# Four buffers for the modulation's weight loads, and its VectorE steps tied to the weight tile they accompany

## Chip, cores and metric

One core of one Trainium2 chip. The metric is the device time of one execution in microseconds (us), median of the runs shown. TensorE (PE) does matmuls, VectorE (DVE) and ScalarE (ACT) elementwise work, GpSimd (POOL) elementwise work and, here, the issue of some DMAs, SyncE (SP) the issue of the others. Each engine works through its own instructions strictly in the order in which they were emitted.

## The reference, cut to what matters

Two transformer blocks over 512 tokens of width 1024, in float32. The part around the change is the conditioning of the second block: for each of its two layers a vector `c` of 1024 numbers gives six modulation vectors of 1024 numbers each.

```python
cond = jax.nn.silu(c)
for i in range(DEPTH):                      # DEPTH = 2
    mod = cond @ ada_w[i] + ada_b[i]        # (1, 1024) @ (1024, 6144)
    sh1, sc1, g1, sh2, sc2, g2 = jnp.split(mod, 6, axis=-1)
    h = modulate(rmsnorm(x, norm1_g[i]), sh1, sc1)
    ...
def sq_relu_mlp(xn, w_up, w_down):
    return jnp.square(jax.nn.relu(xn @ w_up)) @ w_down
```

`ada_w` depends on nothing that the first block computes, so this product can be made at any time before the second block.

## The kernel before

The residual stream is held transposed in eight tiles `h0` to `h7` of 128x512. A weight matrix comes in tiles of 128x1024 (512 KB). For each of them SP issues the load into `wr` (two buffers), ACT makes a rounded copy `wh`, DVE the remainder `wl = wr - wh` (three buffers each), and PE does 24 matmuls of 128x512 (8 blocks of the contraction, each as `xh*wh`, `xl*wh` and `xh*wl`) into one PSUM bank. "Weight tile" below means these 24 matmuls with what belongs to them.

`mlp` (line 675) runs four rounds of 8 up tiles and 8 down tiles, 64 in all. After an up tile DVE computes `t` from PSUM, ACT squares it to `a` and rounds it to `ah`, and DVE makes `al = a - ah`; the eight pairs `ah`, `al` are the moving operands of the following down tiles. After a down tile DVE adds the PSUM bank to `h`. There are four such MLPs; the first two carry a side job.

The side job is `ada` (line 1236), a generator. The matrix `ada_w[i]` has 48 tiles of 128x1024: six groups `q` of eight row blocks `k`. For each, POOL issues a load into an `adaw` buffer (the pool's two), and DVE does two instructions on 128x512 that add `adaw * cs` to the accumulator `ada`. After the eighth of a group DVE transposes `ada` into another `adaw` buffer and reduces it into `red`. At the end 16 small DMAs bring `red` into `part`, and DVE reduces that to `mod`. `mlp` calls the generator once per weight tile, but not at every eighth (`step`, line 681); what is left runs before the last down tiles.

These calls only record instructions. The order in which each engine gets them is made afterwards by `Sched.order` (line 274): a list scheduler that works through estimated times (`cost`, line 243) and, at each moment when an engine is free, hands it the ready instruction that was recorded first. An `ada` step is ready there as soon as its load has landed by those estimates, whatever weight tile PE is at. `Sched.after` (line 194) adds one artificial predecessor, the instruction recorded last, to everything recorded inside it; before, one place in the third layer uses it. All instructions are emitted at line 414, so that they all carry this line in the profile and are told apart by their tiles.

Of the kernel before, what the change touches and what calls it, by code (L numbers as in the profile page):

```python
# [14 lines left out]
ALU = mybir.AluOpType  # L15
AX = mybir.AxisListType
PSUM = bass.MemoryType.PSUM

P = 128
S = 512  # L20
D = 1024
HALVES = slice(0, S // 2), slice(S // 2, S)
KD = D // P
# [15 lines left out]
V_BS = 208  # L39
V_QG, V_KG = 224, 226  # L40
NV = 228


class View:
# [110 lines left out]
class Sched:  # L155
# [37 lines left out]
    @contextmanager  # L193
    def after(self):

        self.gate = len(self.ops) - 1
        yield
        self.gate = None

# [42 lines left out]
    @staticmethod  # L242
    def cost(o, outs, ins):

        ps = any(x.tile.pool.space is not None for x in ins)
        if o.name == "dma_start":
            x = (outs + ins)[0]
            return 1000 if o.eng == "gpsimd" else 60, 1550 + (x.box[1] - x.box[0]) * x.size * 4 / 360
        n = max(x.size for x in outs + ins) if o.name in ("tensor_reduce", "bn_stats", "bn_aggr", "max") else outs[0].size
        if o.eng == "tensor":  # L250
            x = outs[0].size
            if o.name == "matmul" and ins[0].tile.dt == F32:
                return max(64, 4 * 0.42 * x), 200
            return max(107 if o.name == "transpose" else 54, 0.417 * x + 2.5), 200
        if o.eng == "scalar":
            aps = sum(isinstance(o.kw.get(k), View) for k in ("bias", "scale", "accum_out"))
            return (51 if ps else 93) + 0.834 * n + 93 * max(0, aps - 1) + (60 if aps == 1 else 0), 130
        if o.eng == "gpsimd":
            if o.name == "tensor_scalar":
                return 160 if n < 16 else 244 + 0.834 * n, 130  # L260
            if o.name == "memset":
                return 100, 130
            return (300 + 164 * n if n < 16 else 100 + 2.2 * n), 130
        c = 68 + 1.042 * n
        if o.name == "scalar_tensor_tensor" and isinstance(o.args[2], View):
            c += 61
        if o.name == "tensor_scalar" and not ps:
            c = 130 + 0.52 * n
        if o.name == "reciprocal":
            c = 70 + 6.3 * n  # L270
        return c, 130
# [219 lines left out]
class Net:  # L491
# [744 lines left out]
    def ada(self, i):  # L1236
        nc, I = self.nc, self.I

        def side(pool):
            m = self.mod[i]  # L1240
            red, part = (self.t(pool, x, [P, 4, 6 * KD], bufs=1) for x in ("red", "part"))
            for q in range(6):
                acc = self.t(pool, "ada", [P, D])
                for k in range(KD):
                    w = self.t(pool, "adaw", [P, D])
                    nc.gpsimd.dma_start(w, I["ada_w"][i, k, :, q * D : (q + 1) * D])
                    c = self.cs[:, k : k + 1]
                    for s in (0, 512):
                        a = acc[:, s : s + 512]
                        if k == 0:  # L1250
                            nc.vector.tensor_scalar(a, w[:, s : s + 512], c, 1.0, ALU.mult, ALU.mult)
                        else:
                            nc.vector.scalar_tensor_tensor(a, w[:, s : s + 512], c, a, ALU.mult, ALU.add)
                    if k < KD - 1:
                        yield

                tr = self.t(pool, "adaw", [P, D])
                nc.vector.transpose(tr, acc)
                nc.vector.tensor_reduce(red[:, :, q * KD : (q + 1) * KD], tr.rearrange("p (j a k) -> p a j k", a=4, k=32), AX.X, ALU.add)
                yield  # L1260
            for a in range(4):
                for g in range(4):
                    nc.gpsimd.dma_start(part[32 * a : 32 * a + 32, g, :], red[32 * g : 32 * g + 32, a, :])
                yield
            nc.vector.tensor_reduce(m, part.rearrange("p g k -> p k g"), AX.X, ALU.add)
            nc.vector.tensor_tensor(m, m, self.vec[:, V_ADAB[i] : V_ADAB[i] + 48], ALU.add)
            for col, g in ((8, V_N1[i]), (32, V_N2[i])):
                nc.vector.scalar_tensor_tensor(m[:, col : col + 8], m[:, col : col + 8], 1.0, self.vec[:, g : g + 8], ALU.add, ALU.mult)

        return side  # L1270
# [8 lines left out]
    def build(self):  # L1279
        nc, I = self.nc, self.I  # L1280
        self.vec = self.t(self.per, "vec", [P, NV])
        nc.sync.dma_start(self.vec, I["vec"])
# [60 lines left out]
def _consts():  # L1343
    f = np.float32
    half = 32
    inv = 1.0 / (10000.0 ** (np.arange(0, HD, 2, dtype=f) / f(HD)))
    ang = np.arange(S, dtype=f)[:, None] * inv[None, :].astype(f)
    sign = np.concatenate([-np.ones(half, f), np.ones(half, f)])

    def table(a):  # L1350
        c, s = np.cos(a).astype(f).T, np.sin(a).astype(f).T
        c = np.concatenate([c, c])
        s = np.concatenate([s, s]) * sign[:, None]
        return np.stack([np.concatenate([c, c]), np.concatenate([s, s])]).astype(f)

    t = np.arange(S)
    row = (t // 64 - (S // 64) // 2).astype(f)
    col = (t % 64 - 32).astype(f)
    fr = (f(10000.0) ** (-np.arange(16, dtype=f) / f(16))).astype(f)
    ang2 = np.concatenate([row[:, None] * fr, col[:, None] * fr], axis=-1).astype(f)  # L1360
    causal = np.zeros((P, S), f)
    causal[:, S - P :] = np.where(np.arange(P)[None, :] <= np.arange(P)[:, None], 0.0, FAR)
    tri = np.zeros((P, S + 3 * P), f)
    tri[:, 3 * P :] = (np.arange(P)[:, None] <= np.arange(S)[None, :]).astype(f)
    esel = np.zeros((P, 2), f)
    esel[64] = esel[96] = 1.0
    return {"rope_a": table(ang), "rope_c": table(ang2), "causal": causal, "tri": tri, "esel": esel, "ident": np.eye(P, dtype=f)}


def _layout(a):  # L1370
# [61 lines left out]
    r["vec"] = cat(cols, 1)  # L1432
    assert r["vec"].shape == (P, NV)
    r.update(_consts())
# [15 lines left out]
```

## Time and profile before

| | |
|---|---|
| median of 3 runs | 2618.81 us (2616.95 to 2618.96) |
| the profiled execution | 2615.0 us, its span 2613.2 us |
| PE busy | 2544.9 us (97%), 12614 matmuls |
| DVE busy | 1582.8 us (61%) |
| ACT busy | 1169.8 us (45%) |
| POOL busy | 406.6 us (16%) |
| DMA | 290.47 MB, mean 111 GB/s |
| granted TensorE clock, mean | 0.992 |
| `ada` multiply-adds on DVE | 192, from 265.5 to 1050.0 us |
| `adaw` loads | 96 of 512 KB, from 226.3 to 1044.8 us |

The two MLPs with the side job begin near 263 and near 876 us in the span; the other two fill most of the stretches from 1500 to 1800 and from 2300 to 2600 us. In a row of the timeline stand the start, the duration, the engine, the operation with its output and inputs, and in brackets how long the engine had been idle before and what ended that. A matmul's duration overlaps with the next one's, so a rate is read from starts or from counts. In the table of stretches the number in parentheses is the count of instructions.

### The profile page before, as it was taken

The numbers are of one execution on the slowest core, as the hardware profiler recorded it, in microseconds if no ns is written. First come the engines' busy times: TensorE is split into PE (matmuls) and PEld (weight loads), VectorE is DVE, ScalarE is ACT, GpSimd is POOL, SyncE is SP. The second block draws the span as 40 slices with busy tenths as digits, with TensorE's granted clock in tenths as the row PEclk, the third lists the DMA queues.
The fourth block names the chain that finished last, engine by engine and source line by source line (L and its number), as shares of the span: only waits on it lengthen the run. The fifth ranks groups of instructions, "written<-read, shape, count | busy, mean of one in ns | idle before, by whom it ended". The sixth has DMA issues, their size and how long they took to land.

```text
span 2613.2 us, 33470 instructions
## 1 busy us (share of the span) xinstructions
PE 2544.9 (97%) x12614; PEld 2127.2 (81%) x12614; DVE 1582.8 (61%) x2629; ACT 1169.8 (45%) x2104; POOL 406.6 (16%) x453
## 2 busy tenths in 40 slices
PE   7999998999999998999999999999999999999999
PEld 6779786888888886888877888888888888888887
DVE  7998877445578778535698644435447654644433
ACT  5677322335488423324687523323425443523322
POOL 3741112000054111100541200001102110200000
PEclk9999998999999999999999999999999999999999
DMA  4222676333222577332310232222333322233232
GB/s 149 89 69 90 223 227 198 99 96 106 93 74 62 177 231 230 113 97 82 97 57 25 89 97 97 97 97 94 109 105 117 101 95 91 90 99 97 98 97 94
DMA packets 90419, 290.47 MB, mean 111 GB/s; under 512 B 12401, under 2 KB 15729, under 8 KB 90257
## 3 DMA queue, kind: packets, MB, share of 16 engines
q1 hardware_dynamic: 75408, 237.80, 28.3%
q0 software_dynamic: 14848, 50.54, 6.1%
q8 instruction: 99, 1.62, 0.2%
q14 instruction: 64, 0.52, 0.1%
HBM read 277.28 MB, written 2.10 MB: 107 GB/s over the span
## 4 chain that ended last, share of the span: by engine, by line
PE 77%; DVE 10%; DMA 7%; ACT 3%; issue 3%; POOL 0%; SPq 0%; DVEq 0%; ACTq 0%; POOLq 0%
PE mm L414 65%; DMA adaw<-in_ada_w 6%; PE lg L414 4%; PE tp L414 4%; PE po L414 3%; DVE ada L414 2%; DVE mask L414 1%; DVE wl L414 1%; DVE st L414 1%; DVE acc L414 1%; ACT wh L414 0%; DVE xl L414 0%; DVE y L414 0%; DVE o L414 0%; DVE pr L414 0%
## 5 line engine op out<-in xcount | busy, mean ns | idle before, releaser
L414 ACT ACTIVATE wh<-wr 128x1024 fp32r<-128x1024 f32 (+2 forms) x472 | 446.2, 951 | 1022.2 <-PE mm L414 847.3
L414 PE MATMUL mm<-xh,wh 128*128 128x512 f32 (+1 forms) x1640 | 625.7, 382 | 8.3 <-ACT wh L414 8.3
L414 DVE TENSOR_TENSOR wl<-wr,wh 128x1024 fp32r<-128x1024 f32 (+1 forms) x374 | 448.3, 1199 | 301.9 <-ACT wh L414 295.1
L414 PE MATMUL mm<-xh,wl 128*128 128x512 f32 (+1 forms) x1640 | 625.5, 382 | 5.4 <-DVE wl L414 4.8
L414 PE MATMUL mm<-xl,wh 128*128 128x512 f32 (+1 forms) x1640 | 625.0, 381 | 0.7 <-POOL xl L414 0.7
L414 PE MATMUL mm<-ah,wh 128*128 128x512 f32 (+1 forms) x1072 | 409.8, 382 | 13.7 <-ACT ah L414 13.7
L414 PE MATMUL mm<-al,wh 128*128 128x512 f32 (+1 forms) x1072 | 409.8, 382 | 3.6 <-DVE al L414 3.6
L414 PE MATMUL mm<-ah,wl 128*128 128x512 f32 (+1 forms) x1072 | 408.4, 381 | 0.6 <-DVE wl L414 0.6
L414 PEld LDWEIGHTS mm<-xh,wl 128*128 128x128 f32 x1640 | 311.3, 190 | 63.2 <-DVE wl L414 7.7
L414 PEld LDWEIGHTS mm<-xh,wh 128*128 128x128 f32 x1640 | 310.7, 190 | 62.4 <-ACT wh L414 8.7
L414 PEld LDWEIGHTS mm<-xl,wh 128*128 128x128 f32 x1640 | 311.4, 190 | 56.3 <-POOL xl L414 1.4
L414 PEld LDWEIGHTS mm<-ah,wh 128*128 128x128 f32 x1072 | 202.7, 189 | 54.2 <-ACT ah L414 15.8
L414 PEld LDWEIGHTS mm<-al,wh 128*128 128x128 f32 x1072 | 202.7, 189 | 44.5 <-DVE al L414 6.2
L414 DVE SCALAR_TENSOR_TENSOR h<-mm,mod,h 128x512 f32<-128x512 f32 (+1 forms) x113 | 79.9, 708 | 261.8 <-PE mm L414 261.6
L414 PEld LDWEIGHTS mm<-ah,wl 128*128 128x128 f32 x1072 | 202.8, 189 | 39.1 <-DVE wl L414 1.0
L414 POOL TENSOR_TENSOR wl<-wr,wh 128x512 fp32r<-128x512 f32 x98 | 132.5, 1362 | 220.6 <-ACT wh L414 215.8
L414 DVE SCALAR_TENSOR_TENSOR ada<-adaw,cs,ada 128x512 f32<-128x512 f32 x168 | 119.5, 748 | 72.5 <-DMA adaw<-in_ada_w 72.3
L414 ACT ACTIVATE pr<-pr,mn 128x128 f32<-128x128 f32 (+2 forms) x192 | 116.7, 610 | 21.0 <-DVE mn L414 20.2
L414 DVE TENSOR_TENSOR h<-mm,h 128x512 f32<-128x512 f32 (+1 forms) x91 | 56.3, 623 | 108.3 <-PE mm L414 108.2
L414 ACT ACTIVATE ah<-a 128x512 fp32r<-128x512 f32 x128 | 81.0, 632 | 83.8 <-DVE a L414 81.7
L414 DVE TENSOR_TENSOR al<-a,ah 128x512 fp32r<-128x512 f32 x128 | 88.2, 691 | 42.8 <-ACT ah L414 42.8
L414 PE MATMUL tp<-ident,pr 128*128 128x128 f32 x576 | 110.0, 277 | 1.9 <-ACT pr L414 1.0
(260 smaller groups left out, 3795.8 us busy)
## 6 DMA issues: line engine op xcount, KB each, us to landing
adaw<-in_ada_w POOLq DMA_DIRECT2D x96, 512.0 KB, 4.5
wr<-in_w_up SPq DMA_DIRECT2D x64, 512.0 KB
wr<-in_w_down SPq DMA_DIRECT2D x64, 512.0 KB
wr<-in_w_in SPq DMA_DIRECT2D x64, 512.0 KB
wr<-in_w_out SPq DMA_DIRECT2D x64, 512.0 KB
wr<-in_w_gu SPq DMA_DIRECT2D x24, 512.0 KB
wr<-in_w_gv SPq DMA_DIRECT2D x24, 512.0 KB
wr<-in_w_go SPq DMA_DIRECT2D x32, 384.0 KB
```

The costliest lines, as they stand in the source:

```text
L414: getattr(getattr(self.nc, o.eng), o.name)(*args, **kw)
```

## The change

It has three parts. `adaw` gets four buffers (`AW`) in place of the pool's two. A new `Sched.paced(i)` makes instruction `i` a predecessor of what is recorded inside; the multiply-adds of an `ada` step, and the transpose and reduction, are recorded inside it, with `g`, the last instruction recorded before the step. At an up tile that is the DVE instruction that makes `al`, at a down tile the DVE addition to `h`; where a transpose follows directly on the eighth step, it is that step's last instruction. The loads are recorded outside of it. In the scheduler's estimates a DMA issued by POOL now takes 600 ns of POOL (1000 before) and lands 2000 ns later than before; the `ada` DMAs are the only ones issued there.

```diff
+AW = 4
...
     def after(self):
-        self.gate = len(self.ops) - 1
+        with self.paced(len(self.ops) - 1):
+            yield
+
+    @contextmanager
+    def paced(self, i):
+        self.gate = i
         yield
         self.gate = None
...
-            return 1000 if o.eng == "gpsimd" else 60, 1550 + (x.box[1] - x.box[0]) * x.size * 4 / 360
+            late = 1550 + (x.box[1] - x.box[0]) * x.size * 4 / 360
+            return (600, late + 2000) if o.eng == "gpsimd" else (60, late)
...
                 for k in range(KD):
-                    w = self.t(pool, "adaw", [P, D])
+                    g = len(self.sched.ops) - 1
+                    w = self.t(pool, "adaw", [P, D], bufs=AW)
                     nc.gpsimd.dma_start(w, I["ada_w"][i, k, :, q * D : (q + 1) * D])
                     c = self.cs[:, k : k + 1]
+                    with self.sched.paced(g):
-                    for s in (0, 512):
+                        for s in (0, 512):
...
-                tr = self.t(pool, "adaw", [P, D])
-                nc.vector.transpose(tr, acc)
-                nc.vector.tensor_reduce(red[...], tr.rearrange(...), AX.X, ALU.add)
+                g = len(self.sched.ops) - 1
+                tr = self.t(pool, "adaw", [P, D], bufs=AW)
+                with self.sched.paced(g):
+                    nc.vector.transpose(tr, acc)
+                    nc.vector.tensor_reduce(red[...], tr.rearrange(...), AX.X, ALU.add)
```

What this moves, first on DVE, in the second round of up tiles of the first MLP; `adaw_...` is the load that a multiply-add reads, `mm_1110` and `mm_1119` are the PSUM banks of two up tiles that follow each other. Before:

```order
L414 TENSOR_SCALAR ada_1237_4429<-adaw_1238_4397,cs_19_119 128x512
L414 SCALAR_TENSOR_TENSOR t_1111_4438<-mm_1110_4387,y_961_3616 128x512
L414 TENSOR_SCALAR ada_1237_4429<-adaw_1238_4397,cs_19_119 128x512
L414 TENSOR_TENSOR wl_1136_4447<-wr_1134_4366,wh_1135_4433 128x1024
L414 TENSOR_TENSOR al_1114_4458<-a_1112_4444,ah_1113_4453 128x512
L414 SCALAR_TENSOR_TENSOR ada_1237_4429<-adaw_1247_4431,cs_19_119,ada_1237_4429 128x512 x2
L414 SCALAR_TENSOR_TENSOR ada_1237_4429<-adaw_1256_4450,cs_19_119,ada_1237_4429 128x512
L414 SCALAR_TENSOR_TENSOR t_1120_4485<-mm_1119_4435,y_961_3616 128x512
L414 SCALAR_TENSOR_TENSOR ada_1237_4429<-adaw_1256_4450,cs_19_119,ada_1237_4429 128x512
L414 TENSOR_TENSOR wl_1145_4496<-wr_1143_4418,wh_1144_4480 128x1024
L414 TENSOR_TENSOR al_1123_4507<-a_1121_4491,ah_1122_4500 128x512
```

The same two weight tiles with the change:

```order
L423 SCALAR_TENSOR_TENSOR t_1111_4371<-mm_1110_4321,y_961_3603 128x512
L423 TENSOR_TENSOR wl_1136_4380<-wr_1134_4296,wh_1135_4366 128x1024
L423 TENSOR_TENSOR al_1114_4393<-a_1112_4378,ah_1113_4385 128x512
L423 SCALAR_TENSOR_TENSOR ada_1105_4361<-adaw_1115_4317,cs_19_119,ada_1105_4361 128x512 x2
L423 SCALAR_TENSOR_TENSOR t_1120_4415<-mm_1119_4368,y_961_3603 128x512
L423 TENSOR_TENSOR wl_1145_4423<-wr_1143_4353,wh_1144_4411 128x1024
L423 TENSOR_TENSOR al_1123_4433<-a_1121_4421,ah_1122_4428 128x512
L423 SCALAR_TENSOR_TENSOR ada_1105_4361<-adaw_1124_4327,cs_19_119,ada_1105_4361 128x512 x2
```

Before, two to three loads are used up in a weight tile, at any place in it, and here the side job is in its fifth group (`ada_1237`); now exactly one load is used per weight tile, behind `al`, and the side job is in its third group (`ada_1105`). PE's order is the same in both but for one group of four small matmuls in each MLP, and so are ACT's and SP's.

Second on POOL, at the start of the first MLP, before:

```order
L414 DMA adaw_974_3532<-in_ada_w 128x1024
L414 DMA adaw_983_3542<-in_ada_w 128x1024
L414 DMA adaw_992_3583<-in_ada_w 128x1024
L414 TENSOR_TENSOR r_950_3594<-ms_949_3589,mhalf_16_84 128x4
L414 DMA adaw_1001_3605<-in_ada_w 128x1024
```

and with the change:

```order
L423 DMA adaw_974_3532<-in_ada_w 128x1024
L423 DMA adaw_983_3539<-in_ada_w 128x1024
L423 DMA adaw_992_3546<-in_ada_w 128x1024
L423 DMA adaw_1001_3555<-in_ada_w 128x1024
L423 TENSOR_TENSOR r_950_3585<-ms_949_3582,mhalf_16_84 128x4
L423 DMA adaw_1010_3645<-in_ada_w 128x1024
```

Four loads now stand ahead of `r`, the normalization's factor, in place of three; the first four have a buffer each, so that none of them waits for DVE, while before the third waited for DVE to be through with the first.

## Rows read from the trace of the kernel before

**Rows 1.** The page, chain that ended last, shares of the span by line.

```profile
PE mm L414 65%; DMA adaw<-in_ada_w 6%; PE lg L414 4%; PE tp L414 4%; PE po L414 3%; DVE ada L414 2%; DVE mask L414 1%; DVE wl L414 1%; DVE st L414 1%; DVE acc L414 1%; ACT wh L414 0%; DVE xl L414 0%; DVE y L414 0%; DVE o L414 0%; DVE pr L414 0%
```

**Rows 2.** Busy time by stretch: us, then PE, PEld, DVE, ACT, POOL, clock, DMA, GB/s.

```profile
300.00:400.00 100.00, 92.97 (x399) 75.50 (x398) 74.62 (x99) 26.54 (x32) 14.26 (x27) 0.97 0.69 225
400.00:500.00 100.00, 94.41 (x397) 76.80 (x396) 62.19 (x81) 29.73 (x37) 13.75 (x27) 0.94 0.49 158
900.00:1000.00 100.00, 97.33 (x425) 79.14 (x424) 78.65 (x104) 28.35 (x35) 14.45 (x27) 1.00 0.69 226
1000.00:1100.00 100.00, 92.47 (x396) 74.82 (x395) 65.08 (x84) 29.59 (x37) 14.70 (x29) 0.97 0.52 169
500.00:600.00 100.00, 100.00 (x443) 82.84 (x442) 41.09 (x46) 30.68 (x38) 0.00 (x0) 1.00 0.31 100
...
1600.00:1700.00 100.00, 100.00 (x443) 82.81 (x442) 42.39 (x49) 30.91 (x39) 0.00 (x0) 1.00 0.30 97
```

**Rows 3.** PE's waits, 290 to 460 us: us in total, times, longest.

```profile
PE mm L414 <- ACT ah L414: 6.4, 2, 3.3
PE mm L414 <- DVE wl L414: 3.6, 1, 3.6
PE mm L414 <- DVE al L414: 2.4, 2, 1.7
```

**Rows 4.** PE's waits, 890 to 1060 us.

```profile
PE mm L414 <- ACT ah L414: 7.2, 3, 3.8
PE mm L414 <- DVE wl L414: 1.8, 3, 1.0
PE mm L414 <- DVE al L414: 1.2, 3, 0.7
```

**Rows 5.** Timeline of DVE, 386 to 400 us.

```profile
391.51 1.41 DVE L414 SCALAR_TENSOR_TENSOR ada<-adaw,cs,ada 128x512 f32<-128x512 f32 x2 [2.19 <-DMA adaw<-in_ada_w]
396.15 0.75 DVE L414 SCALAR_TENSOR_TENSOR ada<-adaw,cs,ada 128x512 f32<-128x512 f32 x1 [3.23 <-DMA adaw<-in_ada_w]
396.82 0.69 DVE L414 SCALAR_TENSOR_TENSOR t<-mm,y 128x512 f32<-128x512 f32 x1
...
398.08 1.22 DVE L414 TENSOR_TENSOR wl<-wr,wh 128x1024 fp32r<-128x1024 f32 x1
399.21 0.69 DVE L414 TENSOR_TENSOR al<-a,ah 128x512 fp32r<-128x512 f32 x1
```

**Rows 6.** Timeline of POOL, 384 to 403 us.

```profile
387.88 0.53 POOL L414 DMA_DIRECT2D adaw<-in_ada_w  x1 [0.86 <-DVE ada L414]
```

**Rows 7.** Timeline of PE, 394 to 406 us.

```profile
395.34 0.39 PE L414 MATMUL mm<-xl,wh 128*128 128x512 f32 x1
399.35 0.79 PE L414 MATMUL mm<-xh,wl 128*128 128x512 f32 x1 [3.62 <-DVE wl L414]
399.94 0.63 PE L414 MATMUL mm<-xh,wh 128*128 128x512 f32 x1
...
404.21 0.62 PE L414 MATMUL mm<-xl,wh 128*128 128x512 f32 x1
```

**Rows 8.** The tile adaw: duration ns min/median/max, first and last start.

```profile
L414 DVE STREAM_TRANSPOSE adaw<-ada x12: 1235/1245/1246, 294.3 to 1050.7; 128x1024 f32<-128x1024 f32 x12
L414 DVE TENSOR_REDUCE red<-adaw x12: 1199/1211/1220, 296.0 to 1052.0; 128x32 f32<-128x1024 f32 x12
...
DMA to landing us min/median/max: 3.9/4.5/8.2
```

**Rows 9.** The tile part, in the same form.

```profile
L414 POOL DMA_DIRECT2D part<-red x32: 496/496/519, 447.5 to 1061.2; - x32
...
DMA to landing us min/median/max: 1.5/2.7/3.9
```

**Rows 10.** Timeline of SP, 268.5 to 271 us.

```profile
269.99 0.33 SPq L414 DMA_DIRECT2D wr<-in_w_up  x1
```

**Rows 11.** Timeline of ACT, 266 to 281 us.

```profile
276.36 1.06 ACT L414 ACTIVATE wh<-wr 128x1024 fp32r<-128x1024 f32 x1 [2.56 <-DMA wr<-in_w_up]
```

More of the change, by code (lines that the diff above doesn't have):

```diff
@@ L1244, in side @@
                 for k in range(KD):
-                    w = self.t(pool, "adaw", [P, D])
+                    g = len(self.sched.ops) - 1
+                    w = self.t(pool, "adaw", [P, D], bufs=AW)
                     nc.gpsimd.dma_start(w, I["ada_w"][i, k, :, q * D : (q + 1) * D])
                     c = self.cs[:, k : k + 1]
-                    for s in (0, 512):
[L1249 to L1253, printed above, removed]
+                    with self.sched.paced(g):
+                        for s in (0, 512):
+                            a = acc[:, s : s + 512]
+                            if k == 0:
+                                nc.vector.tensor_scalar(a, w[:, s : s + 512], c, 1.0, ALU.mult, ALU.mult)
+                            else:
+                                nc.vector.scalar_tensor_tensor(a, w[:, s : s + 512], c, a, ALU.mult, ALU.add)
                     if k < KD - 1:
                         yield
-                tr = self.t(pool, "adaw", [P, D])
-                nc.vector.transpose(tr, acc)
-                nc.vector.tensor_reduce(red[:, :, q * KD : (q + 1) * KD], tr.rearrange("p (j a k) -> p a j k", a=4, k=32), AX.X, ALU.add)
+                g = len(self.sched.ops) - 1
+                tr = self.t(pool, "adaw", [P, D], bufs=AW)
+                with self.sched.paced(g):
+                    nc.vector.transpose(tr, acc)
+                    nc.vector.tensor_reduce(red[:, :, q * KD : (q + 1) * KD], tr.rearrange("p (j a k) -> p a j k", a=4, k=32), AX.X, ALU.add)
                 yield
```

## The prediction

> **What bounds the kernel now.** I read the views in this order: the chain that ended last, the busy time by stretch, PE's waits in the stretches that stand out, and then single instructions there.
>
> The chain [rows 1] says PE for most of the span and loads of `adaw` for 6%, some 157 us. That is no price. The chain is followed backwards from releaser to releaser, and where DVE waits for a load it runs through DVE even if PE has work at the time. What the loads cost must be read on PE.
>
> The stretches [rows 2] do that. In 500 to 600 and 1600 to 1700 us, MLPs without side work, PE runs 443 matmuls in 100 us at full clock: 0.2257 us each, 5.42 us per weight tile of 24. In 300 to 500 and 900 to 1100 us, with the side job, it runs 399, 397, 425 and 396, though nothing but the same kind of matmul is in them. DVE is at 75% at most there, so it is no lack of DVE time on average. PE's waits [rows 3, 4] name the partners: `wl`, `ah` and `al`, all of them DVE's work or waiting for DVE's work (`ah` comes from `t`).
>
> One such wait can be followed. POOL issued a load at 387.88 [rows 6]; DVE reached the multiply-add that reads it, idled 3.23 us and began at 396.15, more than 8 us after the issue [rows 5]. Behind it in DVE's queue stood `t` and, at 398.08, `wl`. PE had started a matmul at 395.34 and got its next operand only at 399.35, after 3.62 us [rows 7]. From 399.94 to 404.21 it then ran 10 matmuls at 0.427 us each, about half speed: the lower of the clock's two levels (1.2 against 2.4 GHz), as the granted clock of 0.94 on average in 400 to 500 us, against 1.00 in 500 to 600 [rows 2], also says. So a load that is late by a few microseconds stops DVE, DVE holds back a `wl` or `al`, PE stands still, and the restart is slow.
>
> **What the change removes.** No instruction goes; the side job keeps its 192 multiply-adds, 12 transposes, 12 reductions, 96 loads. What goes is DVE's waiting for loads with matmul operands queued behind it.
>
> The gain is the matmuls that are missing against 443: 44 + 46 + 18 + 47 = 155 [rows 2]. At 0.2257 us each that is 35.0 us. Of this PE's waits are 12.4 us in the first MLP [rows 3] and 10.2 us in the second [rows 4], 22.6 together; the other 12.4 us are restarts and matmuls at the lower clock, which go with the waits.
>
> Will the new order have no such wait? **The load.** A step now uses one load per weight tile, and with four buffers the load for the step three ahead is out by then. That is 3 x 5.42 = 16.3 us, and the slowest landing seen is 8.2, the median 4.5 [rows 8]. With two buffers and two to three loads used per tile the time ahead was less than one tile. I price this wait at nothing; its cover is 8 us, and if it were gone DVE would stand still behind `al`, with the next `t` late.
>
> **DVE's time.** An up tile takes at most 0.69 (`t`) + 1.22 (`wl`) + 0.69 (`al`) + 1.41 (the pair of multiply-adds) = 4.0 us [rows 5] of 5.42, a down tile less. Six times in an MLP the transpose and the reduction come on top, 1.25 + 1.21 [rows 8]: 6.5 us, 1.1 more than a tile. The next `t` is then up to 1.1 us late, and the slack of 1.4 us in each other tile takes it up again. `wl` is made for the tile after next or later, so 1.1 us does not reach PE.
>
> **The seam from up to down.** The tightest operand is the last `al` of a round. The first down tile needs it for its 22nd matmul, so 21 x 0.2257 = 4.7 us after the up tiles end. From the start of `t` to the end of `al` it took 3.1 us with one multiply-add in between (396.82 to 399.90) [rows 5]. A whole pair more makes 3.1 + 0.75 = 3.9, under 4.7. Moreover the generator is not called at every eighth tile, so that no pair is recorded for the last up tile of a round, and none of the six transposes falls there (they belong to tiles 9, 18, 27, 36, 45 and 54). Nothing, with 0.8 us of cover.
>
> **POOL and the tail.** POOL's order is loads only, between `r` and the 16 small DMAs. Those now come behind the last reduction, in tile 55 of 64 instead of tile 34 or so: 16 x 0.5 = 8 us of issue and up to 3.9 us to land [rows 9], 12 us. DVE reaches the reduction to `mod` after the residuals of two down tiles, some three tiles or 16 us later. It is in DVE's order ahead of other work, so a late landing would hold that up; the cover is 4 us, and I take nothing.
>
> **SP's loads.** This is the unknown cost, since no row shows `wr` loads beside a load per tile for a whole MLP. Side traffic gets thinner: 225 GB/s in 300 to 400 us now, 100 without it [rows 2]; spread over 55 tiles it is (1 + 7/8) x 0.524 MB / 5.42 us = 181 GB/s. Only at the start of the first MLP is it thicker, with three loads issued together where one was. The bounds: nothing (their `wr` lands in time), and two loads more ahead of one `wr`, 1.05 MB at 225 GB/s, 4.7 us, once per MLP, so 9.4. I take 0.6 for both, near the lower end, because a `wr` is loaded two tiles (10.8 us) before its matmuls and one with two side loads around took 6.4 us from issue (269.99) to the start of `wh` (276.36) [rows 10, 11]. A gain is excluded beyond the 35.0 us.
>
> The Trainium skill (DMA: Bandwidth & Descriptors, Queues, rings and completion order) says that each DMA engine takes turns between the queues that have work for it, a packet at a time. By it a `wr` beside queued side loads would get half of the engines, and more buffers mean that such a time lasts longer; by this rule alone the sum would be no better than its 9.4 us bound. That is the fourth case below.
>
> **The sum.** 2615.0 - 35.0 + 0.6 = 2580.6 us for a profiled execution. The median of the runs, 2618.8, lies 3.8 us above the profiled one. So I predict **2584.4 us**, 1.3% less. A measurement here tells about 0.2% (5.2 us) from no change.
>
> **The rivals.**
> - *As forecast*, 0.82. For: every one of PE's waits in these stretches ends on DVE or on ACT behind DVE, and MLPs without the side job have none. Own range 2580 to 2594: the whole 35.0 us and 2 us less for the scatter of the runs, to the 9.4 us bound.
> - *The seam stays*, 0.11. The last `al` is still late at the four seams of each MLP, say by 2.2 us with its restart. For: all the long waits for `ah` [rows 3, 4] lie at seams. Against: the 0.8 us of cover. Eight times 2.2 is 17.6: 2602.
> - *It does not do what it says*, 0.03. DVE's stalls are moved and not removed, for instance if POOL's issue is so late that three tiles ahead are not kept: near 2618, no difference. Against: POOL has nothing else there.
> - *Slower by starved weight loads*, 0.04. A `wr` buffer goes round in two tiles, 10.8 us: landing, 1.06 of `wh`, 1.22 of `wl`, and some 0.2 for the signals. So the landing may take 8.3 us. Beyond that each microsecond costs half of one in each of 98 tiles, 49 us; from 9.0 us on the gain is eaten, at 9.5 the time is 2584 + 59 = 2643. For: one `adaw` load did take 8.2 us [rows 8], and side loads now run beside all 49 steps of each MLP. Against: the 6.4 us above, at a denser time. The skill's rule of taking turns speaks for this case; the rows so far do not show a `wr` that slow.
>
> **How the numbers follow.** Faster by more than 0.2%: the first two, 0.93. Same 0.03, slower 0.04. The range must leave out at most 0.2: from 2580 to 2597, the first case and the smaller half of the second.
>
> **What would show it.** Right: 443 matmuls at clock 1.00 in every 100 us inside the first two MLPs; DVE's wait for `adaw` near nothing; `ada` steps spread over 55 tiles, to about 560 and 1155 us (the second MLP begins 20 us sooner); POOL's wait for DVE before loads longer. Wrong in size: waits of PE for `ah` at the seams, or for `wh` and `wl` with ACT waiting for `wr` (fourth case). Wrong as a whole: PE at 443 there and the time lost elsewhere, as at the end of an MLP with DVE waiting for `part`.

## The result and the profile after

The changed kernel took 2580.97 us in the median of 4 runs (2579.30 to 2585.20), the kernel before 2617.88 us beside it (4 runs, 2616.51 to 2618.96): a ratio of 0.9862, with a 95% interval of 0.9845 to 0.9879, or 1.4% less. The profiled execution took 2581.65 us with a span of 2579.8 us, which is 33.4 us less than the span before (2613.2 us).

The stretches of the two MLPs with the side job come first (columns as in [rows 2]: us, then PE, PEld, DVE, ACT, POOL, clock, DMA, GB/s).

```profile
300.00:400.00 100.00, 100.00 (x443) 82.81 (x442) 64.54 (x82) 31.47 (x39) 8.45 (x16) 1.00 0.57 183
400.00:500.00 100.00, 100.00 (x443) 82.81 (x442) 65.72 (x84) 28.64 (x35) 8.78 (x17) 1.00 0.55 179
900.00:1000.00 100.00, 100.00 (x443) 82.80 (x442) 65.18 (x83) 30.18 (x37) 7.92 (x15) 1.00 0.56 179
1000.00:1100.00 100.00, 100.00 (x443) 82.78 (x442) 64.54 (x81) 28.38 (x34) 8.97 (x17) 1.00 0.57 180
```

PE has 443 matmuls in each, at full clock, where [rows 2] had 399, 397, 425 and 396; the side job is spread thinner, at 180 GB/s. PE has no wait at all between 270 and 600 us, so nothing answers to [rows 3], and none between 865 and 1190 us for [rows 4]. DVE's waits from 270 to 600 us in the changed kernel (us in total, times, longest) are:

```profile
DVE h L423 <- PE mm L423: 60.9, 26, 2.7
DVE t L423 <- PE mm L423: 42.4, 27, 3.3
DVE wl L423 <- ACT wh L423: 10.2, 39, 3.1
```

The loads of `adaw` are gone from this list: DVE now waits for PE. The chain that ended last, for [rows 1], has lost its `adaw` entry too:

```profile
PE mm L423 76%; PE lg L423 4%; PE tp L423 4%; PE po L423 4%; DVE mask L423 1%; DVE st L423 1%; DVE acc L423 1%; DVE xl L423 0%; DVE pr L423 0%; ACT wh L423 0%; DVE o L423 0%; DVE y L423 0%; DVE m L423 0%; DVE wl L423 0%; ACT st L423 0%
```

The tile `adaw`, for [rows 8]: the transposes last as long as before, the loads land no later, and the side job ends at 1156.1 us in place of 1052.0. POOL now sits 469.5 us before its loads until DVE has freed a buffer.

```profile
L423 DVE STREAM_TRANSPOSE adaw<-ada x12: 1236/1242/1245, 315.5 to 1154.2; 128x1024 f32<-128x1024 f32 x12
L423 DVE TENSOR_REDUCE red<-adaw x12: 1207/1214/1223, 316.7 to 1156.1; 128x32 f32<-128x1024 f32 x12
...
  DVE ada L423: 469.5, 78
...
DMA to landing us min/median/max: 3.9/4.3/6.5
```

**Where the time came from.** DVE drains PSUM into `t` or `h` once per weight tile, so that the same instruction can be found in both traces by its count. From 254 us on there are 255 of them in each. The timeline of DVE, kernel before, has the 1st, the 65th (near the end of the first MLP), the 130th (late in the second) and the last:

```profile
255.70 0.42 DVE L414 TENSOR_TENSOR h<-mm,h 128x256 f32<-128x256 f32 x1
...
622.10 0.69 DVE L414 TENSOR_TENSOR h<-mm,h 128x512 f32<-128x512 f32 x1 [2.08 <-PE mm L414]
...
1191.66 0.69 DVE L414 SCALAR_TENSOR_TENSOR t<-mm,y 128x512 f32<-128x512 f32 x1 [2.69 <-PE mm L414]
...
2609.30 0.75 DVE L414 SCALAR_TENSOR_TENSOR h<-mm,mod,h 128x512 f32<-128x512 f32 x1 [4.69 <-PE mm L414]
```

The same four instructions in the changed kernel:

```profile
254.67 0.42 DVE L423 TENSOR_TENSOR h<-mm,h 128x256 f32<-128x256 f32 x1
...
600.72 0.69 DVE L423 TENSOR_TENSOR h<-mm,h 128x512 f32<-128x512 f32 x1 [2.08 <-PE mm L423]
...
1155.49 0.69 DVE L423 SCALAR_TENSOR_TENSOR t<-mm,y 128x512 f32<-128x512 f32 x1
...
2575.89 0.75 DVE L423 SCALAR_TENSOR_TENSOR h<-mm,mod,h 128x512 f32<-128x512 f32 x1 [4.69 <-PE mm L423]
```

They come 1.03, 21.38, 36.17 and 33.41 us sooner. So the first MLP gave 20.35 us and the stretch with the second 14.79 us, 35.1 together. Behind that 2.8 us were lost again, in stages whose work the change leaves as it was. By the same counting 1.5 us are lost between the 151st and the 161st of these instructions and 1.5 us between the 181st and the 201st. In each of the two stretches PE waits 1.3 us for `acc`, in the kernel before and in the changed one alike, but in the changed one it restarts at a lower granted clock. The changed kernel (columns as above):

```profile
1440.00:1450.00 10.00, 8.67 (x61) 8.47 (x60) 5.22 (x13) 5.06 (x13) 5.27 (x6) 0.83 0.35 106
1795.00:1805.00 10.00, 8.68 (x61) 8.47 (x60) 5.09 (x14) 5.26 (x13) 5.15 (x6) 0.83 0.36 109
```

The same places in the kernel before, 73 matmuls in place of 61:

```profile
1476.00:1486.00 10.00, 8.68 (x73) 8.47 (x72) 5.97 (x16) 6.58 (x16) 6.50 (x8) 1.00 0.30 106
1830.00:1840.00 10.00, 8.68 (x73) 8.48 (x73) 6.16 (x17) 6.26 (x16) 6.33 (x7) 1.00 0.34 108
```

Of the kernels below, the one with the placing alone has the first of these two low stretches and not the second, the one with four buffers alone the second and not the first, and the one with placing and estimates has neither. They go with no part of the change, so I take the 2.8 us for scatter of the profiled executions.

### The profile page after: what moved, and what is told of

Read it like the earlier page. It is cut to its first block, busy times and chain, and to the rows that moved or that the text cites. A ratio compares the mean times of both kernels' runs of the same rounds, so it can differ in the third digit from the quotient of the medians.

```text
span 2579.8 us, 33446 instructions
## 1 busy us (share of the span) xinstructions
PE 2532.9 (98%) x12614; PEld 2124.3 (82%) x12614; DVE 1584.0 (61%) x2629; ACT 1167.4 (45%) x2104; POOL 404.3 (16%) x453
## 4 chain that ended last, share of the span: by engine, by line
PE 88%; DVE 7%; ACT 3%; issue 1%; DMA 1%; POOL 0%; SPq 0%; DVEq 0%; ACTq 0%; POOLq 0%
PE mm L423 76%; PE lg L423 4%; PE tp L423 4%; PE po L423 4%; DVE mask L423 1%; DVE st L423 1%; DVE acc L423 1%; DVE xl L423 0%; DVE pr L423 0%; ACT wh L423 0%; DVE o L423 0%; DVE y L423 0%; DVE m L423 0%; DVE wl L423 0%; ACT st L423 0%
## 5 line engine op out<-in xcount | busy, mean ns | idle before, releaser
L423 POOL DMA_DIRECT2D adaw<-in_ada_w x96 | 51.1, 533 | 532.6 <-DVE ada L423 469.5
L423 ACT ACTIVATE pr<-pr,mn 128x128 f32<-128x128 f32 (+2 forms) x192 | 116.6, 610 | 21.9 <-DVE mn L423 21.1
```

Of the source, the lines that this page charges most:

```text
L423: getattr(getattr(self.nc, o.eng), o.name)(*args, **kw)
```

## Experiments

The change has three parts: the placing, the buffers, the estimates. My first theory (A) was that the placing is what counts. Each experiment was compared with runs of the kernel before on the same chip.

| kernel | us, median | ratio to before (95%) |
|---|---|---|
| placing alone, two buffers | 2584.02 | 0.9869 (0.9851 to 0.9886) |
| placing and estimates, two buffers | 2580.04 | 0.9855 (0.9838 to 0.9872) |
| four buffers alone | 2583.02 | 0.9867 (0.9849 to 0.9886) |
| estimates alone, two buffers | 2580.88 | 0.9860 (0.9839 to 0.9882) |
| order of before, four real buffers | 2581.16 | 0.9862 (0.9845 to 0.9878) |
| order of before, three real buffers | 2581.33 | 0.9867 (0.9851 to 0.9882) |
| estimate further from the truth, two buffers | 2682.49 | 1.0247 (1.0227 to 1.0267) |
| the same order, four real buffers | 2583.36 | 0.9870 (0.9855 to 0.9885) |
| changed kernel, one buffer | 2633.49 | 1.0056 (1.0040 to 1.0073) |
| changed kernel, every multiply-add twice | 2584.63 | one run |
| changed kernel, every load three times | 2579.30 | one run |
| changed kernel, every load five times | 2758.18 | 1.0538 (1.0507 to 1.0569) |

### One part at a time

The kernels are the changed kernel with parts of it undone. Placing alone undoes the buffers and the estimates:

```diff
-AW = 4
+AW = 2
...
-            return (600, late + 2000) if o.eng == "gpsimd" else (60, late)
+            return (1000, late) if o.eng == "gpsimd" else (60, late)
```

> Only the placing of the steps: two buffers and the old cost estimates of before, but every multiply-add, transpose and reduction behind the last VectorE instruction of its weight tile. Theory A (the order is what counts): a load is issued when the step two tiles earlier has freed its buffer, so it has 2 x 5.42 = 10.8 us against landings of 3.9 to 8.2 us in the kernel before; only the first load after each of the 12 transposes has one tile, 5.42 us, against a median landing of 4.5. So DVE waits for adaw under 10 us in all, PE has 443 matmuls in every 100 us from 300 to 500 and from 900 to 1100 us, and the time is 2582 us (2578 to 2590), the whole gain. Theory B (the two further buffers carry the gain): DVE still waits for loads with matmul operands behind them, and at least half of the gain is missing: 2600 to 2618 us, PE under 425 matmuls per 100 us in those stretches.

Placing and estimates with two buffers undoes `AW` only (the first two lines of that diff):

> Placing and the new cost estimates, with two buffers. Theory A: as with the placing alone, 2582 us (2578 to 2590), since the estimates no longer decide where a step stands. Theory B (buffers): 2600 to 2618 us. Theory C (the cost estimates matter on their own): better than the placing alone by over 5 us.

Four buffers alone undoes the estimates (its last two lines) and the placing, at both places:

```diff
-                    with self.sched.paced(g):
+                    with ExitStack():
```

> Four buffers with the order left to the scheduler and the old cost estimates. In its order DVE takes 4.1 multiply-adds per weight tile on average (up to 6) until the 24th tile of the first MLP is over, against 3.2 before. Theory A (the order is what counts): the loads are now asked for at 2 per 5.42 us tile, and DVE's up tile is 0.69 + 1.22 + 0.69 + 4.1 x 0.75 = 5.7 us, over the tile's 5.42; so PE still waits for wl, ah and al in a shorter stretch, and the time is 2605 us (2592 to 2622), less than half of the gain. Theory B (buffers): with four loads under way DVE no longer waits, and the time is 2580 to 2588 us with 443 matmuls per 100 us.

Estimates alone undoes `AW` and the placing, in the same lines:

> Only the scheduler's estimates of DMAs issued by POOL (600 ns of issue, landing 2000 ns later); two buffers, no placing. In the order DVE takes 2.5 multiply-adds per tile on average, between 0 and 4, over 39 tiles, against 3.2 over 29 before. Theory A: fewer late loads but still some, with operands queued behind them: 2603 us (2590 to 2614), PE between 410 and 440 matmuls per 100 us. Theory C (a truer estimate is enough): 2580 to 2588 us. Rival (no effect): 2612 to 2620 us.

All four gave the whole gain; their intervals overlap with each other and with that of the full change. For the placing theory A held, but for the buffers alone it fell: 2605 us was expected and 2583 measured. It fell for the estimates as well (2603 against 2581). Theory C of the second kernel was not borne out: with the estimates added to the placing the time was 4.0 us lower, not over 5, and the two intervals overlap. So no single part carries the gain. Any one of the three is enough.

The stretches of four buffers alone show what had been wrong in my reason:

```profile
300.00:400.00 100.00, 100.00 (x442) 82.79 (x442) 97.16 (x133) 33.72 (x41) 18.49 (x35) 1.00 0.83 285
...
900.00:1000.00 100.00, 100.00 (x443) 82.81 (x442) 94.07 (x125) 30.13 (x37) 21.34 (x41) 1.00 0.79 264
```

DVE is busy 97% of the time, with up to six multiply-adds in a weight tile, and PE loses nothing. I had counted DVE's work and found it over a tile; it fits, barely. DVE's time is not what PE lost, nor is the place of a multiply-add in DVE's queue, as long as DVE isn't standing still. DVE's waits between 300 and 400 us, kernel before:

```profile
DVE ada L414 <- DMA adaw<-in_ada_w: 24.0, 20, 3.2
...
DVE h L414 <- PE mm L414: 0.6, 1, 0.6
```

The same in four buffers alone:

```profile
DVE ada L423 <- DMA adaw<-in_ada_w: 2.0, 3, 0.9
```

In the kernel before DVE was busy for 74.6 us of that stretch [rows 2] and stood before loads for 24.0: 98.6 of 100 us were gone, and it waited for PE only 0.6 us. It had become the bound, at 75% busy.

### Supply against demand

The second theory: the loss is the rate at which `adaw` buffers deliver loads, set against the rate at which the order uses them. POOL's loads from 300 to 400 us, kernel before (us busy, mean ns, idle before and its releasers):

```profile
L414 POOL DMA_DIRECT2D adaw<-in_ada_w x27 | 14.3, 528 | 86.7 <-DVE ada L414 78.2 <-DVE red L414 8.5
```

That is 27 loads in 100 us, one every 3.7 us, each issued when DVE had freed a buffer. The order used 1.6 to 2 per weight tile of 5.42 us, one every 2.7 to 3.4 us: in the first MLP DVE does the 96 multiply-adds in 29 tiles, 3.3 per tile, and never more than four, that is two loads, in one. The estimates alone lower the demand (2.5 multiply-adds per tile, 1.25 loads, one every 4.3 us), the placing lowers it to 7 loads in 8 tiles, and the buffers raise the supply: 35 loads in the first stretch of four buffers alone.

To test it, the scheduler kept its two buffers, so that the order of every engine's instructions is that of before, and only the real buffers were raised:

```diff
     def place(self):
...
-            tag, bufs = (self.tag, self.bufs) if p.shared is None else ("all", p.shared + len(p.slots))
+            tag, bufs = (self.tag, 4 if self.tag == "adaw" else self.bufs) if p.shared is None else ("all", p.shared + len(p.slots))
```

> The kernel before with its instruction order on every engine kept as it is, and four real adaw buffers in place of two, so that a load waits for the step four before it. Theory A (the loss was the rate at which two buffers deliver, under what the order asks for): two buffers gave a load every 3.7 us, the order asks for 1.6 to 2 per tile of 5.42 us, one every 2.7 to 3.4; with four under way the loads come at twice the rate, DVE's waits for adaw fall from 41 and 32 us to under 8 per MLP, PE has 443 matmuls per 100 us, 2582 us (2577 to 2590). Rival (the order itself holds operands back, the loads only show it): 2600 us or more with PE waiting for wl, ah and al.

With three:

> The same with three real buffers. Theory A: 3.7 x 2/3 = 2.5 us per load, just faster than the 2.7 that the order asks for at most, so nearly all of the gain: 2584 us (2578 to 2594), DVE waiting 5 to 20 us per MLP for adaw. Rival (it takes all four): 2600 us or more.

Both gave the whole gain, with no instruction moved: in the traces the operations of PE, DVE, ACT and POOL follow each other in the sequence of the kernel before. In the kernel with four real buffers, 300 to 400 us:

```profile
300.00:400.00 100.00, 100.00 (x443) 82.81 (x442) 88.58 (x117) 30.67 (x38) 15.83 (x30) 1.00 0.77 256
```

With three, DVE's waits for loads from 270 to 600 us:

```profile
DVE ada L423 <- DMA adaw<-in_ada_w: 2.9, 3, 1.2
```

So the order of before, with its multiply-adds at any place, costs PE nothing if the loads are there.

The opposite was tried by one number in the kernel before, a landing estimate 1500 ns lower, so that the order uses more loads per tile from the same two buffers (here `late` is the estimate of before):

```diff
-            return (1000, late) if o.eng == "gpsimd" else (60, late)
+            return (1000, late - 1500) if o.eng == "gpsimd" else (60, late)
```

> The kernel before with one number changed: the scheduler believes that POOL's loads land 1500 ns sooner than it believed, further from the truth. Its order then takes 3.6 multiply-adds per weight tile over 27 tiles of the first MLP, against 3.2 over 29 before, still with two buffers. Theory A: two buffers deliver a load every 3.7 us (27 loads in 100 us in the kernel before), so 1.8 loads per tile take 6.7 us where a tile lasts 5.42; over 27 tiles that is up to 34 us per MLP against 20 by the same sum before. The time is 2632 us (2620 to 2655), and DVE busy and waiting for loads fills all of the stretch from 300 to 400 us. Rival (the loss in the kernel before is bound to a few unlucky places, such as the seams, and not to the rate): 2600 to 2620 us.

It took 2682.49 us. Its stretches:

```profile
300.00:400.00 100.00, 80.62 (x317) 63.27 (x317) 61.18 (x82) 18.75 (x22) 11.61 (x22) 0.90 0.58 189
400.00:500.00 100.00, 83.90 (x334) 66.58 (x333) 60.37 (x82) 25.35 (x31) 15.92 (x31) 0.90 0.50 164
...
900.00:1000.00 100.00, 88.18 (x371) 70.92 (x370) 65.83 (x90) 28.10 (x38) 13.12 (x23) 0.93 0.55 181
1000.00:1100.00 100.00, 75.97 (x297) 58.59 (x296) 64.95 (x87) 22.78 (x29) 12.32 (x23) 0.90 0.59 195
```

DVE's waits from 300 to 400 us:

```profile
DVE ada L423 <- DMA adaw<-in_ada_w: 38.7, 15, 4.2
```

Busy and waiting make 61.2 + 38.7 = 99.9 of 100 us. The matmuls missing against 443 are 126 + 109 + 72 + 146 = 453, at 0.2257 us each 102 us; the span is 2684.4 - 2579.8 = 104.6 us over the changed kernel's. The direction and the place were right, and the size was not: I had taken the 3.7 us per load as fixed, and it was 4.5 here (22 loads in 100 us). That the same two buffers deliver more slowly when DVE and PE hold each other up agrees with this, since a load is only issued once DVE is through with an earlier one. The transfers themselves were hardly slower: in this stretch a load landed after 4.7 us in the median, against 4.5 before. What grew is POOL's wait for a free buffer, 87.6 us over 22 loads (4.0 us each) against 86.7 over 27 (3.2).

The same order with four real buffers, by the edit to `place` above:

> The slow kernel with the optimistic estimate, its order of instructions kept on every engine, with four real buffers. Theory A (delivery against demand): the order asks for 1.8 loads per tile, one every 3.0 us, and four buffers deliver one every 1.9 to 2.9 (35 in 100 us with four buffers alone); the 65 us that this order cost with two buffers vanish, and it is 2583 us (2577 to 2595). Rival (an order made from a wrong estimate costs time whatever the buffers): 2620 us or more.

2583.36 us: the 99 us that this order costs with two buffers are gone with four.

### One buffer

```diff
-AW = 4
+AW = 1
```

> The changed kernel with one adaw buffer. Now every load is issued only when the pair of multiply-adds before it is through, so one round of load and pair takes 0.53 (issue) + 4.3 (landing) + 1.41 (pair) + signals, about 6.4 us, more than a weight tile's 5.42, and DVE stands waiting for a load again, about 1 us at nearly every one of the 48 steps, 50 us per MLP, more than the 41 and 32 us of the kernel before. But the order has at most three steps in tiles that follow each other and then one without, and each wait stands behind al. Theory A (what counts is whether the loads come as fast as the order uses them, over a few tiles): the lateness of some 1 us per step is made good in the tiles without a step, PE loses 0 to 8 us per MLP, 2588 us (2578 to 2600). Rival (the sum of DVE's waits for loads is what PE loses): 2615 us or more.

The time, 2633.49 us, is the rival's, but its reason is not. The stretches inside the first MLP and at its end:

```profile
300.00:400.00 100.00, 100.00 (x442) 82.81 (x442) 62.72 (x77) 32.23 (x41) 6.33 (x12) 1.00 0.50 162
...
600.00:700.00 100.00, 81.84 (x418) 68.98 (x417) 56.90 (x89) 38.96 (x64) 13.08 (x24) 0.90 0.39 120
```

Inside the MLPs PE keeps its pace, and DVE waits for loads only 8.5 us from 270 to 620 and 6.1 us from 870 to 1190. I had expected 50 for each MLP; but the scheduler knew of the one buffer and set only 44 of the 48 steps into the 64 tiles of the first MLP. So the side job wasn't through when that MLP ended. DVE's last steps:

```profile
636.01 1.40 DVE L423 SCALAR_TENSOR_TENSOR ada<-adaw,cs,ada 128x512 f32<-128x512 f32 x2
645.00 1.42 DVE L423 SCALAR_TENSOR_TENSOR ada<-adaw,cs,ada 128x512 f32<-128x512 f32 x2 [7.59 <-DMA adaw<-in_ada_w]
646.45 1.25 DVE L423 STREAM_TRANSPOSE adaw<-ada 128x1024 f32<-128x1024 f32 x1
647.73 1.22 DVE L423 TENSOR_REDUCE red<-adaw 128x32 f32<-128x1024 f32 x1
```

After these came the `part` DMAs, for which DVE waited 9.6 us, while PE waited once for 18.1 us (for `wh`) from 600 to 720 us and once for 17.3 us (for `v`) from 1190 to 1330 us, and restarted at a lower clock (0.90 on average between 600 and 700 us). These two waits are 35.4 of the 52.5 us by which this kernel is slower than the changed one; the rest I did not take apart. This is the danger of spreading a side job thinly: here it ran past the end of its cover. In the changed kernel the last `part` DMAs begin soon enough: the first at 564.8 us, and DVE reads them at 581.0 without a wait.

```profile
L423 POOL DMA_DIRECT2D part<-red x32: 496/498/519, 564.8 to 1165.3; - x32
L423 DVE TENSOR_REDUCE mod<-part x2: 478/484/489, 581.0 to 1173.8; 128x48 f32<-128x192 f32 x2
```

### The seam and the weight loads

For the seam from up to down tiles, every multiply-add was done twice, the second into an accumulator that nothing reads:

```diff
                                 nc.vector.scalar_tensor_tensor(a, w[:, s : s + 512], c, a, ALU.mult, ALU.add)
+                            b = acb[:, s : s + 512]
+                            if k == 0:
+                                nc.vector.tensor_scalar(b, w[:, s : s + 512], c, 1.0, ALU.mult, ALU.mult)
+                            else:
+                                nc.vector.scalar_tensor_tensor(b, w[:, s : s + 512], c, b, ALU.mult, ALU.add)
```

> The changed kernel with every multiply-add done twice, the second time into an accumulator that nothing reads. DVE has 0.69 + 1.22 + 0.69 + 2.82 = 5.4 us of work in an up tile, the whole tile, and less in a down tile. Seam: from the start of t to the end of the last al with two multiply-adds more in between it is 3.1 + 0.75 + 1.41 = 5.3 us where 4.7 are there. Theory A: DVE holds the pace on average, as it did at 97% busy with four buffers alone; if the pairs come between t and al of a round's last up tile, PE waits 0.6 us for ah or al at each of the 7 seams of an MLP; time 2584 us (2578 to 2594). Rival (a seam has no such margin, the case that I gave 0.11): 2600 us or more, PE waiting for ah or al 1 us and more at every seam.

```profile
300.00:400.00 100.00, 100.00 (x443) 82.83 (x442) 86.18 (x118) 32.41 (x39) 8.44 (x16) 1.00 0.57 184
```

DVE goes from 65% to 86% busy and PE has no wait between 270 and 620 us. But the doubled work did not come where I feared it. At the first seam DVE does this:

```profile
312.25 0.68 DVE L423 SCALAR_TENSOR_TENSOR t<-mm,y 128x512 f32<-128x512 f32 x1
312.86 1.21 DVE L423 TENSOR_TENSOR wl<-wr,wh 128x1024 fp32r<-128x1024 f32 x1
314.30 0.69 DVE L423 TENSOR_TENSOR al<-a,ah 128x512 fp32r<-128x512 f32 x1 [0.23 <-ACT ah L423]
```

At all eight seams of the two MLPs only `wl` stands between the last `t` of a round and its last `al`, here as in the changed kernel; the doubled pair stands ahead of `t`. At five of the eight it makes `t` late, by up to 1.3 us, and the last `al` still ends 1.0 us or more before the matmul that reads it, against 2.0 us in the changed kernel. So the seam bears twice the work ahead of it. A whole pair between `t` and `al` was not tried. In the kernel with four buffers alone one multiply-add stands there at the first seam, with `t` late as well, and 1.1 us are left.

For the weight loads, every `adaw` load was issued three times or five times, with the added lines below standing there twice or four times:

```diff
                     nc.gpsimd.dma_start(w, I["ada_w"][i, k, :, q * D : (q + 1) * D])
+                    with self.sched.paced(g):
+                        x = self.t(pool, "adax", [P, D], bufs=AW)
+                        nc.gpsimd.dma_start(x, I["ada_w"][i, k, :, q * D : (q + 1) * D])
```

> The changed kernel with every adaw load issued three times, twice into buffers that nothing reads; DVE's work is as in the changed kernel. Traffic in the first two MLPs is (1 + 3 x 7/8) x 0.524 MB / 5.42 us = 350 GB/s. With four buffers alone 285 GB/s kept the DMA engines busy 83% of the time, so 350 is 102%: just over what they can do. Theory A (queues share, weight loads suffer with the side loads): a tile then takes 1.02 x 5.42 = 5.53 us or more, PE waits for wh and wl with ACT waiting for wr, and the time is 2600 us (2585 to 2660). Rival (weight loads take precedence or have enough of a share whatever the side load does): PE keeps 443 matmuls per 100 us and the side loads fall behind until DVE waits for adaw; 2578 to 2590 us if DVE's waits stay short, with landings of adaw of 8 us and more.

```profile
300.00:400.00 100.00, 100.00 (x443) 82.81 (x442) 64.64 (x82) 31.75 (x39) 25.72 (x49) 1.00 0.93 357
400.00:500.00 100.00, 100.00 (x443) 82.81 (x442) 65.70 (x83) 28.37 (x34) 25.71 (x49) 1.00 0.93 348
```

Twice the traffic of the changed kernel, and PE misses nothing; the tile `adaw` in this kernel lands later, but not late for its place:

```profile
DMA to landing us min/median/max: 3.8/6.4/9.0
```

ACT's waits for `wr` are 17.3 us in all from 270 to 600 us, and none reaches PE. The rival held, theory A's 2600 us did not.

> The changed kernel with every adaw load issued five times, four of them into buffers that nothing reads. The traffic asked for in the first two MLPs is (1 + 5 x 7/8) x 0.524 MB / 5.42 us = 520 GB/s, more than any stretch of these runs moved (375 GB/s in the busiest slice with triple loads), so that something must fall behind; the question is which. Theory A (the weight loads get what they ask for, 97 GB/s, and the side loads the rest): the side loads get at most 278 GB/s, a step then takes 5 x 0.524 / 278 = 9.4 us, DVE waits for adaw with t, wl and al behind it, and PE loses through DVE: a tile lasts some 7/8 x 9.4 = 8.3 us over 55 tiles in each of two MLPs, up to 300 us more, 2750 to 2950 us; ACT waits for wr under 30 us per MLP. Theory B (weight loads are starved, the case that I gave 0.04): PE's waits are for wh, and ACT waits for wr several microseconds in most tiles, over 100 us per MLP, while DVE does not wait for adaw.

```profile
300.00:400.00 100.00, 85.37 (x369) 69.91 (x367) 48.14 (x60) 24.33 (x30) 32.60 (x63) 0.95 1.01 389
400.00:500.00 100.00, 75.43 (x305) 61.00 (x306) 48.38 (x63) 20.28 (x24) 29.42 (x56) 0.84 0.99 380
```

The DMA engines are full here, at 380 to 389 GB/s, and the time is 2758.18 us. Who waits, from 270 to 690 us, first PE:

```profile
PE mm L423 <- DVE wl L423: 53.5, 5, 15.4
PE mm L423 <- DVE al L423: 9.3, 2, 9.0
PE mm L423 <- ACT ah L423: 6.3, 3, 2.2
```

Then DVE and ACT:

```profile
DVE ada L423 <- DMA adaw<-in_ada_w: 110.9, 8, 26.0
DVE wl L423 <- ACT wh L423: 52.3, 29, 6.0
...
ACT wh L423 <- DMA wr<-in_w_up: 111.5, 23, 27.3
```

PE's waits go by way of DVE, as in theory A; none is for `wh`. ACT does wait for `wr`, more than theory A allowed. Much of that follows from DVE, because SP waited 299.9 us for `wl` to free a `wr` buffer before it could issue the next load. But the 52.3 us of `wl` behind `wh` are loads of weights that landed late on a full DMA, and how much of PE's loss they are stays open. DVE's longest wait for `adaw`, 26.0 us, is more than the 12.9 us that the slowest of these loads took to land: the load was also issued late, since POOL stood 243.1 us from 270 to 690 us before the added loads, whose own four buffers were not free.

## Why the prediction was right, and where its reasons were not

**The sum.** 35.0 us were forecast from 155 missing matmuls, 90 in the first MLP (20.3 us) and 65 in the second (14.7). Measured: 20.35 and 14.79. Counting matmuls against a stretch without the side job gave the price, with waits and restarts in one; the chain's 6%, some 157 us, did not. The other side of the sum fits as well: 22.6 us of it were PE's waits and 12.4 us were put down to the lower clock, and the clocks in [rows 2] (0.97, 0.94, 1.00 and 0.97) are 3 + 6 + 0 + 3 = 12 us short of full speed. The 0.6 us for late `wr` loads was not there; even at 357 GB/s PE kept 443.

**The total.** For the profiled execution 2580.6 us were forecast, and it took 2581.65: the MLPs gave what was expected, and the stages after them 2.8 us less. The step that failed is the 3.8 us by which I moved the sum to the median. That distance is scatter of one execution of before, whose runs on other chips spread from 2612.05 to 2624.43; the changed kernel's profiled run lay 0.7 us above its median. So the median, 2580.97, came 3.4 us under the forecast of 2584.4.

It lies inside the range, but near its lower end, and that end does not follow from its words: the median less the whole 35.0 us and 2 us more is 2618.8 - 35.0 - 2 = 2581.8, not 2580. By the sum as it stands the result would lie 0.8 us below, so that 2580 held is luck.

**The load's cover.** The forecast of no wait was right. The 3 x 5.42 us of four buffers was more than was needed: the placing alone has the whole gain with two. "Two to three loads used per tile" for the kernel before is too much. A tile touches up to three loads, but it uses up 1.65 on average and two at most in the first MLP.

**DVE's time.** "75% at most" is a misreading: in 900 to 1000 us it is 79% [rows 2]. The conclusion, that DVE has time enough on average, was too quick in any case. In that stretch DVE was busy for 78.7 us and waited 21.9 us for loads, so it was full.

**The mechanism.** "A load that is late stops DVE, and DVE holds back a `wl` or `al`" holds, and the last six lines of DVE's order of before, under "The change", are the instructions of [rows 5] (one is left out there), in the same sequence, with the two waits for a load among them. What the prediction did not ask is which part removes the wait: it reckoned with one load per tile and four buffers together. My theory A, after the result, took the order for the cause. The experiments show supply against demand: with the order of before unchanged, one more buffer was enough.

**The rivals.** The seam (0.11) did not stay, and its cover was larger than the 0.8 us of the prediction. That number allowed for a pair between `t` and the last `al`, where only `wl` stands (the prediction says itself that no pair is recorded there), and took the 22nd matmul as the one that needs `al`, where it is the 23rd. At each of the eight seams of the changed kernel `al` ends 2.75 us after the start of `t` and 2.04 us before that matmul. "Does not do what it says" (0.03) did not happen; no load wait moved elsewhere. Weight loads so starved that PE waits (0.04) were not seen at 181 GB/s nor at 352.

By that last rival the Trainium skill (DMA: Bandwidth & Descriptors, Queues, rings and completion order) had been read as speaking against the change, since the DMA engines take turns between queues that have work. Read with the numbers it speaks for it: the weights' queue asks for 97 of 352 GB/s, less than half, so that turns would give it all it asks. PE's 443 matmuls with triple loads agree with that. The run with five loads does not settle it: there the weights ask for no more, and ACT waited 153.3 us for `wr` from 270 to 690 us, partly because SP could issue only late.

**Signs.** 443 at clock 1.00: yes. DVE's wait for `adaw`: none in the first MLP. Side job to about 560 and 1155 us: `part` begins at 564.8, and the last reduction is at 1156.1. POOL's wait for DVE is longer: 469.5 us against 288.6.

## What to carry to other kernels

For a side stream through a ring of buffers, compare two rates: how often the consuming engine's order uses a load, and how often the ring delivers one (count the issues in a stretch). Where demand is over supply, an engine that looks 75% busy is full, and it holds up whatever else stands in its queue; here a further buffer, a thinner order and a truer estimate each cured it, and one of them was enough. Then look at the end of the stream: spread too thinly it runs past its cover.

## What was not expected of the hardware

- The same two buffers delivered a load every 3.7 us in one order and every 4.5 us in another (27 and 22 in 100 us): a ring's rate is no constant of its size.
- DVE at 97% busy, with multiply-adds among the operands that it makes for PE, cost PE nothing, and 24 us of waiting at 75% busy cost it 44 matmuls in the same 100 us.
- Weight loads stayed in time for PE beside side loads up to 357 GB/s in all (DMA share 0.93), though ACT waited 17.3 us for them in 330; at 380 to 389 GB/s the share was 0.99 to 1.01, side loads took 9.1 us in the median to land (4.3 in the changed kernel), and PE lost time.
